# Forgetting attention with its causal mask in the maximum's VectorE pass instead of mask matmuls, and memory tokens multiplied by their factor row at load

## The chip, the cores and the metric

The kernel runs on one core of a Trainium2 chip. A core has a matrix engine (TensorE, PE in the profile; its weight loads are listed as PEld), VectorE (DVE), ScalarE (ACT), GpSimd (POOL) and the queue that issues its transfers (SyncE, SP), which run side by side and wait for one another through semaphores. The time is that of one execution on the device in microseconds. TensorE multiplies a stationary 128x128 tile, loaded as weights, with a moving tile of up to 512 columns; results are summed in PSUM, which has eight banks of 128x512 float32. SBUF is the core's working memory; "DRAM" below means the large memory behind the DMAs.

## The reference, cut to what matters

One decoder layer on 1024 tokens of 1024 features. Four mLSTM heads and eight heads of forgetting attention read the same normalised input; then follow cross-attention into 256 memory tokens and a squared-ReLU MLP. The two parts that the change touches:

```python
def rmsnorm(x, g):
    y = xf * lax.rsqrt(jnp.mean(xf * xf, axis=-1, keepdims=True) + EPS)
    return (y * g.astype(jnp.float32)).astype(x.dtype)

def forgetting_attention(q, k, v, lf):          # per block of 128 queries
    s = jnp.einsum('bqhd,bkhd->bhqk', qi, k) * scale
    s = s + (ci[..., :, None] - cT[..., None, :])
    s = jnp.where(qpos[:, None] >= kpos[None, :], s, -jnp.inf)
    p = jax.nn.softmax(s, axis=-1)
    return jnp.einsum('bhqk,bkhd->bqhd', p.astype(v.dtype), v)

# cross-attention's keys and values, with h = rmsnorm(mem, ln_mem):
k, v = jnp.split(memn @ w_kv, 2, axis=-1)
```

## The kernel before

All activations lie with features on the partitions: x is [128, 8, 1024], eight blocks of 128 features by 1024 tokens. Every float32 product is made of three matmuls on halves: `split` makes a high part (an ACT copy into the matmul's format, L132 or, with a scale, L135) and the remainder as a low part (a DVE subtraction, L133, or with a scale L136), and `mm3` issues low x high, high x low and high x high (L184, L185, L186).

The stages in order: the first norm and the first values (0 to about 63 us), the mLSTM heads with their input projections (to about 380), forgetting attention (about 358 to 600), output projection, cross-attention and MLP (to the end). Outside forgetting attention a planner of the program builder sets each engine's order. It weighs when operands and buffers are ready; `tc.issue_after` only sets the earliest place. Buffers come from small pools: `w2(tag)` hands out [128, 512] tiles, one or two of each tag, and a tile is handed out again only when the last reader of its former content is done. PSUM tiles go by tags too: three `sc`, one `mm`, one `m2`, two `tp`, one `ov`.

**Forgetting attention** is made of tiles of 128 queries (`Tile`) by up to 1024 keys, in one part up to 512 keys and in two beyond. There are 64 tiles (8 heads x 8 blocks), and their last parts have 128, 256, 384 or 512 columns, 16 of each; 32 tiles have a first part of 512 as well. Each part goes through `score` (two matmuls, L721 and L722, and on a tile's last part a third, L724, which adds the causal mask to the last 128 columns by multiplying a bf16 identity with a bf16 mask), `top` (the negated maximum, L728, on DVE; with two parts also the smaller of the two, L731), `exp` (the exponential on ACT, straight from PSUM, with that maximum as its bias), and `scale` (the division by the sum: L741 and L742 on DVE, the product on POOL). `Values` then turns 128-column pieces of the result (L760, TensorE), splits them and multiplies them with the values (L779).

The order here is written by hand: `slot` issues, for one step, the turn of one piece, the products of an earlier one, the maxima of the part scored in the slot before, the piece's split, the exponentials of the part before that, and the scores of the next part; the rest of the slot is filled with matmuls of other work. `in_order` chains each engine's instructions in the order in which they were written. The filler is made of units: cross-attention's keys (`key_unit`, 8 of them) and values (`value_unit`), and half of the output projection. A key unit's matmuls end in a `sink` that multiplies by the factor row of the memory tokens (L874) into SBUF and, in the slot after, splits; a value unit's sink splits straight out of PSUM, scaled by a factor column (L896).

**The memory tokens** are read by `mem_prepare`, which is called ahead of the mLSTM heads and so planned among them (its loads are issued at 14.8 and near 41 us, the last one, of the row, at 86). It reads four pieces of 128x512 (two blocks of 128 features by 256 tokens each), sums their squares, splits them with their gain and stores both halves to DRAM (`hmd`), from where the filler reads them. From the sums come the norm's factors, as a column (`rcol_m`) and, through `to_row`, as a row copied to all partitions (`row_m`): a transpose on TensorE, an ACT copy, a store to DRAM (L249) and a load that repeats the row (L251).

What stands around it on the queues there: `ml_project` of the first head convolves the keys (`conv_silu`, L495 to L503: the projection's PSUM times a row, four taps of 128x1024 on DVE, L498 and L500, and the gate, L503), projects forgetting attention's queries (`fx_project`, 2 x 24 matmuls, whose results go through DVE, L631), transposes the convolved keys (L516 in `carried`, whose result DVE reads at L518), and convolves the queries (24 matmuls for each half).

## Time and profile before

| | |
|---|---|
| median of 3 runs | 1556.06 us (1556.05 to 1556.83) |
| span of the profiled execution | 1551.3 us |
| TensorE busy | 1512.5 us, 97% |
| VectorE busy | 1115.3 us, 72% |
| ScalarE busy | 721.7 us, 47% |
| GpSimd busy | 474.4 us, 31% |
| DMA | 311.94 MB, 201 GB/s mean |

The span is the time from the first to the last instruction that the profiler recorded, for one execution; the profiled execution has no time of its own beside the span, and the runs' times hold about 5 us more than it, the start and the end of the program. In a timeline a row is: start, duration, engine, line, operation, output<-inputs, shape, and in brackets how long the engine stood idle before it and for whom. "SPq" is the queue that issues transfers. A matmul's duration is its latency: the next one starts before it ends, so what one costs is the step to the start of the next. The same holds, to a smaller degree, on VectorE.

The busy share of each engine in 40 slices of the span, with TensorE's granted clock in tenths:

```profile
PE   8999999999999999999999999989999999999997
DVE  7666676665789874944457988888877777767666
ACT  7324343334787763634443556556555422211234
PEclk9999999999999999999999999999999999999998
```

TensorE is busy in nine tenths or more of nearly every slice. VectorE stands at eight or nine tenths in slices 11 to 14, which are forgetting attention (a slice is 38.8 us).

### The profile page before, as it was taken

The numbers are of one execution on the slowest core, as the hardware profiler recorded it, in microseconds if no ns is written. First come the engines' busy times: TensorE is split into PE (matmuls) and PEld (weight loads), VectorE is DVE, ScalarE is ACT, GpSimd is POOL, SyncE is SP. The second block draws the span as 40 slices with busy tenths as digits, with TensorE's granted clock in tenths as the row PEclk, the third lists the DMA queues.
The fourth block names the chain that finished last, engine by engine and source line by source line (L and its number), as shares of the span: only waits on it lengthen the run. The fifth ranks groups of instructions, "written<-read, shape, count | busy, mean of one in ns | idle before, by whom it ended". The sixth has DMA issues, their size and how long they took to land. (4 is left out here: it accounts for less than half of the span.)

```text
span 1551.3 us, 22016 instructions
## 1 busy us (share of the span) xinstructions
PE 1512.5 (97%) x7729; PEld 1262.4 (81%) x7729; DVE 1115.3 (72%) x1736; ACT 721.7 (47%) x1351; POOL 474.4 (31%) x515
## 2 busy tenths in 40 slices
PE   8999999999999999999999999989999999999997
PEld 8878888889898887788888787777777878888887
DVE  7666676665789874944457988888877777767666
ACT  7324343334787763634443556556555422211234
POOL 0003030413455441511110034444444633333320
PEclk9999999999999999999999999999999999999998
DMA  6422223436878949943344457777777976666623
GB/s 220 122 78 84 99 99 113 130 130 170 253 252 231 296 165 312 321 156 117 115 156 154 145 178 265 277 276 260 269 251 261 387 288 244 238 245 239 243 93 110
DMA packets 122108, 311.94 MB, mean 201 GB/s; under 512 B 13566, under 2 KB 28216, under 8 KB 114060
## 3 DMA queue, kind: packets, MB, share of 16 engines
q1 hardware_dynamic: 121996, 310.52, 57.7%
q8 instruction: 61, 1.00, 0.3%
q14 instruction: 51, 0.42, 0.1%
HBM read 206.42 MB, written 104.05 MB: 200 GB/s over the span
## 5 line engine op out<-in xcount | busy, mean ns | idle before, releaser
L184 PE MATMUL tp<-act,wl 128*128 128x512 f32 (+1 forms) x448 | 177.5, 396 | 6.9 <-DVE r_f L1326 3.8
L185 PE MATMUL tp<-act,wh 128*128 128x512 f32 (+1 forms) x448 | 176.3, 393 | 0.0
L186 PE MATMUL tp<-act,wh 128*128 128x512 f32 (+1 forms) x448 | 175.9, 394 | 0.0
L133 DVE TENSOR_TENSOR wl<-wr,wh 128x1024 fp32r<-128x1024 f32 (+2 forms) x99 | 129.1, 1304 | 27.4 <-ACT wh L132 27.0
L132 ACT ACTIVATE wh<-wr 128x1024 fp32r<-128x1024 f32 (+2 forms) x99 | 99.0, 1000 | 86.8 <-PE tp L186 37.2
L184 PE MATMUL mm<-act,wl 128*128 128x512 f32 (+1 forms) x336 | 130.7, 389 | 3.0 <-DVE r_e L1071 1.5
L186 PE MATMUL mm<-act,wh 128*128 128x512 f32 (+1 forms) x336 | 129.0, 384 | 0.0
L185 PE MATMUL mm<-act,wh 128*128 128x512 f32 (+1 forms) x336 | 128.8, 383 | 0.0
L184 PE MATMUL m<-act,wl 128*128 128x512 f32 (+1 forms) x312 | 120.5, 386 | 1.8 <-DVE wl L133 1.5
L186 PE MATMUL m<-act,wh 128*128 128x512 f32 (+1 forms) x312 | 119.3, 382 | 0.0
L185 PE MATMUL m<-act,wh 128*128 128x512 f32 (+1 forms) x312 | 119.1, 382 | 0.0
L184 PEld LDWEIGHTS tp<-act,wl 128*128 128x128 f32 x448 | 84.7, 189 | 28.0 <-DVE r_f L1326 4.2
L184 PE MATMUL sc<-act,wl 128*128 128x512 f32 (+1 forms) x252 | 99.2, 394 | 5.3 <-DVE r_f L1326 3.4
L186 PEld LDWEIGHTS tp<-act,wh 128*128 128x128 f32 x448 | 84.7, 189 | 19.5
L1410 POOL TENSOR_TENSOR z<-wr 128x256 f32<-128x256 f32 x56 | 50.7, 924 | 161.9 <-DMA wr<-w_ff2q 146.2
L185 PEld LDWEIGHTS tp<-act,wh 128*128 128x128 f32 x448 | 84.8, 189 | 18.8
L132 ACT ACTIVATE w<-wr 128x768 fp32r<-128x768 f32 (+2 forms) x31 | 25.6, 826 | 157.5 <-PE tp L186 90.1
L185 PE MATMUL sc<-act,wh 128*128 128x512 f32 (+1 forms) x252 | 98.5, 391 | 0.0
L186 PE MATMUL sc<-act,wh 128*128 128x512 f32 (+1 forms) x252 | 98.3, 390 | 0.0
L132 ACT ACTIVATE wh<-z 128x1024 fp32r<-128x1024 f32 (+1 forms) x54 | 55.4, 1027 | 56.0 <-POOL z L1410 22.2
L133 DVE TENSOR_TENSOR wl<-z,wh 128x1024 fp32r<-128x1024 f32 (+1 forms) x54 | 73.5, 1362 | 6.1 <-ACT wh L132 5.9
L184 PEld LDWEIGHTS mm<-act,wl 128*128 128x128 f32 x336 | 63.3, 188 | 16.9 <-DVE r_e L1071 1.9
(676 smaller groups left out, 4242.1 us busy)
## 6 DMA issues: line engine op xcount, KB each, us to landing
act<-right SPq DMA_DIRECT2D x49, 1024.0 KB
right<-w SPq DMA_DIRECT2D x56, 256.0 KB
wr<-w_ff2q SPq DMA_DIRECT2D x28, 512.0 KB
right<-r_d SPq DMA_DIRECT2D x49, 256.0 KB
right<-r_e SPq DMA_DIRECT2D x49, 256.0 KB
act<-fqk SPq DMA_DIRECT2D x48, 256.0 KB
wr<-w_in SPq DMA_DIRECT2D x20, 512.0 KB
wr<-w_ff SPq DMA_DIRECT2D x20, 512.0 KB
```

What stands on the lines that cost most here:

```text
L132: s.activation(hi, src, AF.Copy)
L133: return v.tensor_tensor(out=lo, in0=src, in1=hi.bitcast(F32), op=ALU.subtract)
L184: nc.tensor.matmul(ps, w[1], x[0], start=first, stop=False, skip_group_check=more)
L185: nc.tensor.matmul(ps, w[0], x[1], start=False, stop=False, skip_group_check=more)
L186: nc.tensor.matmul(ps, w[0], x[0], start=False, stop=last, skip_group_check=more)
L1410: g.tensor_tensor(out=o, in0=x, in1=y, op=op)
```

## The change

It does three things.

1. The mask matmul (L724) and its bf16 identity go. The mask constant becomes 512 columns wide, zero but for its last 128. On a tile's last part `top` is one `tensor_tensor_reduce` on DVE: it adds the mask's last columns (as many as the part has) to the scores in PSUM, multiplies by -1, writes the result back over the scores and keeps the minimum, starting from the first part's result where there is one. The exponential of such a part takes scale -1. The separate minimum (L731) goes.
2. `mem_prepare` runs in two passes: it loads the four pieces and sums squares; makes the factor columns and the row, which is now a `w2("y")` tile; then loads the four pieces again, multiplies them by gain and row in one DVE operation for each half, and splits and stores them.
3. With the factor inside the memory tokens, the key sink is a split straight from PSUM, without the multiplication and without the slot in between, and the value sink splits without a scale.

```diff
@@ -117,11 +117,9 @@
     g.memset(ident, 1.0)
     g.affine_select(out=ident, in_=ident, pattern=[[-1, P]], compare_op=ALU.is_equal, fill=0.0, base=0, channel_multiplier=1)
     BF16 = mybir.dt.bfloat16
-    identb = const("identb", [P, P], BF16)
-    v.tensor_copy(identb, ident)
-    causal = const("causal", [P, P], BF16)
+    causal = const("causal", [P, TH], BF16)
     g.memset(causal, 0.0)
-    g.affine_select(out=causal, in_=causal, pattern=[[-1, P]], compare_op=ALU.is_ge, fill=-BIG, base=0, channel_multiplier=1)
+    g.affine_select(out=causal, in_=causal, pattern=[[-1, TH]], compare_op=ALU.is_ge, fill=-BIG, base=TH - P, channel_multiplier=1)
     half = const("half", [P, 8])
     g.memset(half, -0.5)
     vec = const("vec", [P, a["vec"].shape[1]])
@@ -274,24 +272,29 @@
     vxd = dram.tile([XH, P, 2, 2, NM], F32, name="vxd")
 
     hmd = dram.tile([P, 2, KT, NM], F32, name="hmd")
-    row_m = const("row_m", [P, NM])
-    rcol_m = const("rcol_m", [P, 2])
 
     def mem_prepare():
         acc = w2("b")
+        pairs_of = lambda t: t.rearrange("p (k c) -> p k c", k=2)
         for i in range(KT // 2):
             raw = w2("f")
-            load(raw.rearrange("p (k c) -> p k c", k=2), a["mem"][:, 2 * i : 2 * i + 2])
+            load(pairs_of(raw), a["mem"][:, 2 * i : 2 * i + 2])
             square_sum(acc, raw, i == 0)
+        cols = col("fac", 2)
+        rsqrt_sums(acc, cols, 2, 2)
+        row_m = w2("y")[:, :NM]
+        to_row(row_m, cols, 2, rowd[1:2, :NM])
+        for i in range(KT // 2):
+            raw = w2("f")
+            load(pairs_of(raw), a["mem"][:, 2 * i : 2 * i + 2])
             hi = w2("p", dt=F32R)
             for e in range(2):
                 c = slice(e * NM, e * NM + NM)
                 gain = vec[:, VEC["ln_mem"] + 2 * i + e :][:, 0:1]
-                split(hi[:, c], raw[:, c].bitcast(F32R), raw[:, c], gain)
+                v.scalar_tensor_tensor(out=raw[:, c], in0=raw[:, c], scalar=gain, in1=row_m, op0=ALU.mult, op1=ALU.mult)
+            split(hi, raw.bitcast(F32R), raw)
             for p_, t in enumerate((hi.bitcast(F32), raw)):
-                load(hmd[:, p_, 2 * i : 2 * i + 2], t.rearrange("p (k c) -> p k c", k=2))
-        rsqrt_sums(acc, rcol_m, 2, 2)
-        to_row(row_m, rcol_m, 2, rowd[1:2, :NM])
+                load(hmd[:, p_, 2 * i : 2 * i + 2], pairs_of(t))
 
 
     xa = act(F32)
@@ -719,19 +722,28 @@
             c2 = max(c1, c0 + 256)
             sp = sc()
             nc.tensor.matmul(sp[:, : c2 - c0], qs2[:, it], kl[:, c0:c2], start=True, stop=False)
-            nc.tensor.matmul(sp[:, : c2 - c0], qs[:, it], kh[:, c0:c2], start=False, stop=c1 < self.wid)
-            if c1 == self.wid:
-                nc.tensor.matmul(sp[:, c1 - c0 - P : c1 - c0], identb, causal, start=False, stop=True)
+            nc.tensor.matmul(sp[:, : c2 - c0], qs[:, it], kh[:, c0:c2], start=False, stop=True)
             self.ps.append(sp[:, : c1 - c0])
 
         def top(self, e):
-            v.tensor_reduce(out=self.mxs[:, e : e + 1], in_=self.ps[e], axis=mybir.AxisListType.X, op=ALU.max, negate=True)
-            if e:
-
-                v.tensor_tensor(out=self.mxs[:, 1:2], in0=self.mxs[:, 0:1], in1=self.mxs[:, 1:2], op=ALU.min)
+            ps = self.ps[e]
+            if e + 1 < len(self.parts):
+                v.tensor_reduce(out=self.mxs[:, e : e + 1], in_=ps, axis=mybir.AxisListType.X, op=ALU.max, negate=True)
+            else:
+
+                v.tensor_tensor_reduce(
+                    out=ps,
+                    in0=ps,
+                    in1=causal[:, TH - ps.shape[1] :],
+                    scale=-1.0,
+                    scalar=self.mxs[:, 0:1] if e else BIG,
+                    op0=ALU.add,
+                    op1=ALU.min,
+                    accum_out=self.mxs[:, e : e + 1],
+                )
 
         def exp(self, e):
-            s.activation(self.pt[:, slice(*self.parts[e])], self.ps[e], AF.Exp, bias=self.mxs[:, e : e + 1], accum_out=self.dens[:, e : e + 1])
+            s.activation(self.pt[:, slice(*self.parts[e])], self.ps[e], AF.Exp, bias=self.mxs[:, e : e + 1], scale=1.0 if e + 1 < len(self.parts) else -1.0, accum_out=self.dens[:, e : e + 1])
             if e:
                 s.activation(self.mxs[:, 0:1], self.mxs[:, 0:1], AF.Exp, bias=self.mxs[:, 1:2], scale=-1.0)
 
@@ -870,14 +882,9 @@
                 yield 1.5, k == KT - 1, lambda: sink(ps)
 
         def sink(ps):
-            t = rotate("p", "a").rearrange("p (e c) -> p e c", e=2)
-            v.tensor_tensor(out=t[:, 1], in0=ps[:, :NM], in1=row_m, op=ALU.mult)
-
-            def store():
-                split(t[:, 0].bitcast(F32R), t[:, 1].bitcast(F32R), t[:, 1])
-                load(kxd[n // 2, :, :, n % 2], t)
-
-            return store
+            t = rotate("p", "a").bitcast(F32R).rearrange("p (e c) -> p e c", e=2)
+            split(t[:, 0], t[:, 1], ps[:, :NM])
+            load(kxd[n // 2, :, :, n % 2], t.bitcast(F32))
 
         return [a["w_xk"][n]], run
 
@@ -893,7 +900,7 @@
 
         def sink(t, ps):
             o = rotate("p", "a").bitcast(F32R).rearrange("p (e c) -> p e c", e=2)
-            split(o[:, 0], o[:, 1], ps, rcol_m[:, t : t + 1])
+            split(o[:, 0], o[:, 1], ps)
             load(vxd[hd, :, :, t], o.bitcast(F32))
 
         return [a["w_xv"][hd, i] for i in range(2)], run
```

Line numbers in the changed program differ by a little: L516, L518, L503 and L631 of before are L519, L521, L506 and L634, L728 is L731, and `split`'s subtraction L133 is L131; `mm3` is L182 to L184. The new DVE pass is L734, the multiplication of a memory piece L294.

In the instruction rows below, names carry a running number for each buffer, and the brackets list whom an instruction waits for.

VectorE in forgetting attention, three tiles of the second half of a head. Before, each part has a reduction, and a two-part tile a minimum:

```order
L728 TENSOR_REDUCE c_mx_3235<-sc_3237 128x1 [waits PE_49]
L742 RECIPROCAL c_den_3212<-c_den_3212 128x1
L136 SCALAR_TENSOR_TENSOR r_b_3655<-tp_3630,rcol,r_b_3655 128x4x64 [waits Activation_49]
L728 TENSOR_REDUCE c_mx_3246<-sc_3248 128x1 [waits PE_49]
L742 RECIPROCAL c_den_3226<-c_den_3226 128x1
L728 TENSOR_REDUCE c_mx_3246<-sc_3255 128x1 [waits PE_49]
L731 TENSOR_TENSOR c_mx_3246<-c_mx_3246 128x1 [waits DVE_49]
L742 RECIPROCAL c_den_3236<-c_den_3236 128x1 [waits Activation_49]
```

VectorE at the same place after the change:

```order
L734 ISA sc_3240,c_mx_3238<-sc_3240,causal 128x512 [waits PE_49]
L734 ISA c_mx_3238 128x1
L754 RECIPROCAL c_den_3217<-c_den_3217 128x1
L134 SCALAR_TENSOR_TENSOR r_b_3648<-tp_3623,rcol,r_b_3648 128x4x64 [waits Activation_49]
L731 TENSOR_REDUCE c_mx_3248<-sc_3250 128x1 [waits PE_49]
L754 RECIPROCAL c_den_3230<-c_den_3230 128x1
L734 ISA sc_3257,c_mx_3248<-sc_3257,causal,c_mx_3248 128x128 [waits DVE_49,PE_49]
L734 ISA c_mx_3248 128x1
L754 RECIPROCAL c_den_3239<-c_den_3239 128x1 [waits Activation_49]
```

The last part's reduction is the pair L734, a pass over the scores and an accumulator read; the first part's reduction stays, and the minimum is gone.

TensorE from the end of `fx_project` of the first head on (its last matmul writes a `tp` bank). Before; `m_113` is the bank of the query convolution, `mm_988` that of the transposed keys, `mm_1095` that of a later projection:

```order
L186 MATMUL tp_952<-act_91,wh_916 128x512
L184 MATMUL m_113_1028<-act_89,wl_1023 128x512 [waits DVE_49]
L185 MATMUL m_113_1028<-act_90,wh_1022 128x512
...
L516 MATMUL mm_988<-ident,z_91_905 128x128 [waits DVE_49]
L516 MATMUL mm_988<-ident,z_91_905 128x128 x3
L184 MATMUL mm_1095<-act_89,wl_1092 128x512 [waits DVE_49]
```

TensorE there after the change, where these banks are `m_119`, `mm_994` and `mm_1101`:

```order
L184 MATMUL tp_958<-act_87,wh_922 128x512
L519 MATMUL mm_994<-ident,z_97_911 128x128 [waits DVE_49]
L519 MATMUL mm_994<-ident,z_97_911 128x128 x3
L182 MATMUL mm_1101<-act_85,wl_1098 128x512 [waits DVE_49]
L183 MATMUL mm_1101<-act_86,wh_1097 128x512 [waits Activation_49]
...
L534 MATMUL tp_1005<-ones,r_c_999 128x1 x4
L182 MATMUL m_119_1034<-act_85,wl_1029 128x512 [waits DVE_49]
```

The query convolution's first block of 24 matmuls, which stood between the projection and the key transposes, now follows a later projection.

VectorE at the same place. Before, between the last tap of the key convolution (`z_91_905`) and the operation that frees the transposes' bank (L518):

```order
L500 SCALAR_TENSOR_TENSOR z_91_905<-z_88_851,vec,z_91_905 128x1024 [waits DVE_49]
L503 SCALAR_TENSOR_TENSOR z_91_905<-z_88_851,z_91_905 128x1024 [waits Activation_49]
L631 SCALAR_TENSOR_TENSOR r_p_977<-tp_952,row 128x512 [waits DMAHW5_49,DMAHW3_49,PE_49]
L133 TENSOR_TENSOR wl_1174<-wr_1171,wh_1173 128x1024 [waits DMAHW1_49,Activation_49]
L136 SCALAR_TENSOR_TENSOR w_84_844<-z_91_905,w_83_843 128x1024 [waits Activation_49]
L133 TENSOR_TENSOR r_p_977<-r_p_977,r_p_979 128x512 [waits Activation_49]
L495 TENSOR_TENSOR z_112_1026<-m_113_1028,row 128x512 [waits PE_49]
L518 TENSOR_TENSOR r_c_993<-mm_988,c_m_984 128x512 [waits PE_49]
```

VectorE there after the change (`r_f` are the pieces of the memory tokens, `r_y` the factor row):

```order
L503 SCALAR_TENSOR_TENSOR z_97_911<-z_94_857,vec,z_97_911 128x1024 [waits DVE_49] x3
L294 SCALAR_TENSOR_TENSOR r_f_811<-r_f_811,vec,r_y_805 128x256 [waits DMAHW6_49,DMAHW5_49,Activation_49]
...
L294 SCALAR_TENSOR_TENSOR r_f_820<-r_f_820,vec,r_y_805 128x256
L506 SCALAR_TENSOR_TENSOR z_97_911<-z_94_857,z_97_911 128x1024 [waits Activation_49]
L131 TENSOR_TENSOR r_f_811<-r_f_811,r_p_813 128x512 [waits Activation_49]
L131 TENSOR_TENSOR r_f_820<-r_f_820,r_p_822 128x512 [waits Activation_49]
L521 TENSOR_TENSOR r_c_999<-mm_994,c_m_990 128x512 [waits PE_49]
```

Four multiplications of memory pieces, which wait for the row's load, now stand ahead of the key convolution's gate (L506), and two splits of pieces ahead of L521; the results of `fx_project` (L631 before) have moved behind them.

## The prediction

> **What bounds the kernel now.** I read the page's first part, then the windows (busy time of each engine in the stage that changes), then TensorE's own waits, longest first.

> ```profile
> span 1551.3 us, 22016 instructions
> PE 1512.5 (97%) x7729; PEld 1262.4 (81%) x7729; DVE 1115.3 (72%) x1736; ACT 721.7 (47%) x1351; POOL 474.4 (31%) x515
> ```

> ```profile
> core 0: us, PE busy (x) PEld busy (x) DVE busy (x) ACT busy (x) POOL busy (x), PEclk, DMA share, GB/s
> 410.00:560.00 150.00, 148.68 (x1014) 130.73 (x1013) 130.13 (x318) 117.55 (x325) 76.39 (x119) 1.00 0.80 245
> ```

> ```profile
> PE mm L184 <- DVE wl L133: 6.9, 1, 6.9
> PE m L184 <- DVE act L136: 1.2, 1, 1.2
> PE mm L184 <- DVE r_c L518: 0.9, 1, 0.9
> ```

> TensorE is the bound: 1512.5 of 1551.3 us, and in the core of forgetting attention 148.68 of 150. The stage is packed: what leaves TensorE's queue there shortens the kernel, unless the engine behind it cannot follow. That one is VectorE: 130.13 of 150, so 20 us are idle. TensorE's waits are few: 6.9 us at the very start, which the change leaves alone, and two of about 1 us, at 46.98 and 95.17, both beside the memory work that is rewritten. The median of the runs, 1556.06, is 4.8 us above this profiled span; I make the sum against the span and add the same 4.8 us.

> **Term 1, the mask products go.** 64 bf16 matmuls of 128 columns, one behind each tile's last score part. First the group, then two pieces of TensorE's timeline: a part without mask and a part with it.

> ```profile
> L724 PE MATMUL sc<-causal,identb x64: 229/229/233, 358.7 to 564.7; 128*128 128x128 bf16 x64
> ```

> ```profile
> 455.60 0.39 PE L722 MATMUL sc<-act 128*128 128x512 f32 x1
> 455.83 0.28 PE L184 MATMUL m<-act,wl 128*128 128x256 f32 x1
> 455.94 0.28 PE L185 MATMUL m<-act,wh 128*128 128x256 f32 x1
> ...
> 466.77 0.40 PE L722 MATMUL sc<-act 128*128 128x512 f32 x1
> 467.01 0.23 PE L724 MATMUL sc<-causal,identb 128*128 128x128 bf16 x1
> 467.05 0.36 PE L184 MATMUL m<-wh,act 128*128 128x256 f32 x1
> 467.25 0.28 PE L185 MATMUL m<-wl,act 128*128 128x256 f32 x1
> ```

> The group's 229 ns is a latency, and matmuls overlap, so I don't multiply by it (64 x 0.229 = 14.7 us would be too much). What the mask costs the queue is the step from L722's start to the second matmul behind it. Without mask: 455.94 - 455.60 = 0.34. With mask: 467.25 - 466.77 = 0.48. Between pairs of equal widths I find 0.13 us. 64 x 0.13 = 8.3; a few masks stand ahead of value transposes, which wait for their weight load anyway, so I count 61: **-7.9 us**. Bounds: 0, if TensorE then waits for VectorE instead, and -14.7.

> **Term 2, VectorE takes the mask over.** Each last part's maximum becomes one pass that adds the mask, negates, writes back and takes the minimum; the built program issues two instructions for it, the pass and a 128x1 read of its accumulator. The 32 first parts keep their reduction, and the 32 small minimum operations (L731) go, since the first part's result enters as the starting value. No row of before shows the new pass. The nearest rows, by form in the window 400 to 590 and in the timeline:

> ```profile
> L728 DVE TENSOR_REDUCE c_mx<-sc 128x1 f32<-128x512 f32 x42 | 28.6, 681 | 0.2
> L133 DVE TENSOR_TENSOR r_e<-tp,r_d 128x512 fp32r<-128x512 f32 x32 | 21.9, 685 | 6.5 <-ACT r_d L132 6.2
> L136 DVE SCALAR_TENSOR_TENSOR r_a<-m,rcol_m,r_a 128x256 fp32r<-128x256 f32 x4 | 1.9, 484 | 0.3 <-ACT r_a L135 0.3
> L874 DVE TENSOR_TENSOR r_a<-m,row_m 128x256 f32<-128x256 f32 x4 | 1.6, 408 | 0.0
> ```

> ```profile
> 441.56 0.16 DVE L731 TENSOR_TENSOR c_mx<-c_mx 128x1 f32<-128x1 f32 x1
> 441.63 0.55 DVE L133 TENSOR_TENSOR r_e<-tp,r_d 128x384 fp32r<-128x384 f32 x1
> ...
> 442.43 0.40 DVE L874 TENSOR_TENSOR r_p<-mm,row_m 128x256 f32<-128x256 f32 x1
> 442.75 0.68 DVE L728 TENSOR_REDUCE c_mx<-sc 128x1 f32<-128x512 f32 x1
> 443.35 0.41 DVE L133 TENSOR_TENSOR r_e<-tp,r_d 128x256 fp32r<-128x256 f32 x1
> ```

> A reduction from PSUM (681 ns) and a two-source operation with one source in PSUM (685) cost the same at 512 columns, and the next one starts 0.60 us after either. So I price the pass like the reduction that it replaces. A 128x1 operation takes its neighbour 0.07 us (441.56 to 441.63); a column operand adds 0.06 to 0.08 (484 against 408 at 256 columns). Balance over the stage: 64 accumulator reads x 0.07 = +4.5 (with 0.16, the full latency, +10); 32 starting columns x 0.06 = +1.9; 32 minima x 0.07 = -2.2; that is +4, at most +10. Eight key sinks lose the multiplication by the row (0.32 each, 442.43 to 442.75) and keep their split, -2.6; value sinks lose a column operand, -0.4. Net about +1 us on an engine with 20 idle. The idle time covers it; if that cover were gone, each us more on VectorE would be a us on the kernel. What is left is delay: the exponential starts one accumulator read later (0.1 us), and the key sink's split now reads PSUM twice, so its bank is free one ScalarE copy later (about 0.3 us), where a column of matmuls waits. I take **+0.5** (0 to +1.5) of new waits.

> **The half-rate bound.** If the pass ran at half rate it would take another 0.33 us on a mean tile (320 of 512 columns x 0.53 us, where 0.53 is what 512 columns take within 0.60). 47 of the 64 tiles lie in the 150 us (64 x 150/206): +15.5 on VectorE, while the window shrinks by 47 x 0.13 = 6. 130 + 15.5 + 4 = 150 in 144: VectorE would be the bound. The turning point is 20/47 = 0.43 us per tile, accumulator read included. The row of a two-source pass that has both sources in SBUF speaks against half rate:

> ```profile
> 38.51 0.88 DVE L136 SCALAR_TENSOR_TENSOR r_f<-r_f,vec,r_p 128x256 fp32r<-128x256 f32 x2
> ```

> Two of them take 0.88, 0.40 or so each from start to start, near the 0.33 with a PSUM source. But none of these rows has an accumulator. [...]

> **Term 3, the memory preparation in two passes.** Before: 4 loads, each squared and split at once. Now: 4 loads and squares; then the factor row (a transpose, a 1 KB store, a broadcast load); then 4 more loads, 8 multiplications by gain and row on VectorE, 4 splits, 8 stores. That adds 4 loads of 256 KB on SP's queue, 8 x 0.40 us on VectorE and exchanges 16 half-width operations for 8 full ones. None of it is needed before forgetting attention, 250 us later; what counts is what stands behind it on VectorE's queue. These rows are TensorE at 44 to 96 us, SP, and what a load takes from issue to its first user:

> ```profile
> 46.98 0.38 PE L184 MATMUL m<-wh,act 128*128 128x256 f32 x1 [1.16 <-DVE act L136]
> ...
> 87.80 0.39 PE L186 MATMUL tp<-act,wh 128*128 128x512 f32 x1
> ...
> 93.62 0.60 PE L516 MATMUL mm<-ident,z 128*128 128x128 f32 x4
> ...
> 95.17 0.50 PE L184 MATMUL mm<-act,wl 128*128 128x512 f32 x1 [0.94 <-DVE r_c L518]
> ```

> ```profile
> 40.35 0.33 SPq L284 DMA_DIRECT2D r_f<-mem  x1
> ...
> 84.32 0.26 SPq L249 DMA_DIRECT2D rowd<-row_m  x1
> ...
> 85.98 0.32 SPq L251 DMA_DIRECT2D row_m<-rowd  x1
> ...
> 179.64 0.33 SPq L251 DMA_DIRECT2D r_a<-facd  x1
> ...
> 195.30 0.32 SPq L634 DMA_DIRECT2D fqk<-r_p  x1
> ```

> ```profile
> 44.31 0.63 ACT L220 ACTIVATE r_c<-r_f 128x512 f32<-128x512 f32 x1 [2.07 <-DMA r_f<-mem]
> ```

> ```profile
> 87.39 1.23 DVE L503 SCALAR_TENSOR_TENSOR z<-z,z 128x1024 f32<-128x1024 f32 x1 [1.19 <-ACT z L502]
> ...
> 182.76 0.75 DVE L618 SCALAR_TENSOR_TENSOR r_f<-r_f,vec,r_a 128x512 f32<-128x512 f32 x1 [2.03 <-DMA r_a<-facd]
> ...
> 197.40 0.69 DVE L631 SCALAR_TENSOR_TENSOR r_p<-m,row 128x512 f32<-128x512 f32 x1 [1.40 <-DMA fqk<-r_p]
> ```

> So a memory load takes 4.0 us (40.35 to 44.31), a broadcast row 3.1 (179.64 to 182.76), a store before its buffer may go 2.1 (195.30 to 197.40).

> At 46.98 the wait came from a memory piece that was loaded late, since its buffers had to come free; with pass 1 only squaring, it is loaded earlier, and the wait should go: 1.16 plus the restart, **-1.3** (0 to -1.4).

> At 88 us the order is worse than before. Then a block of 24 matmuls (the query convolution's, 88.03 to 93.6) stood between forgetting attention's query projection and the transposes L516 of the convolved keys, so VectorE had 5.6 us to finish these keys. Now the transposes (L519 in the new numbering) come directly behind the projection, and VectorE has, ahead of the operation that they wait for, four of the new multiplications, which wait for the broadcast row. The factor columns come about 2 us earlier than before (they stand ahead of one 128x1024 pass that they had followed), so the row's load is issued near 83.9 (1.66 after its store, as 84.32 to 85.98) and lands near 87.0; 4 x 0.40 to 88.6, then the 128x1024 pass (1.23 at 87.39) to 89.9. TensorE, at the end of its projection at 88.0, waits 1.9. Then the transposes' consumer stands behind two splits of 0.60 each: 1.5 lost in place of 1.1. The block that was the cover follows later, and needs a PSUM bank that VectorE's L634 frees, which stands behind the third and fourth memory piece: store issued at 90.3, load at 92.3, landed at 96.3, two pieces multiplied and L634 done at 100.4, against TensorE's arrival near 99: 1.4 (0.7 to 1.7). Perhaps one wait more behind it, 0 to 1.5. Together 1.9 + 0.4 + 1.4 and 0 = **+3.5** after rounding down (0, if the loads come a little earlier, to +6). VectorE's queue, not the DMAs, carries the cost: SP is idle most of this time.

> **The sum.** -7.9 + 0.5 - 1.3 + 3.5 = -5.2. Span 1551.3 - 5.2 = 1546.1, with 4.8 outside 1550.9: I say 1551.0.

> **The clock.** A long wait can cost more than itself: behind a wait of 2.78 us a 512-column matmul took 0.67 in place of 0.39, and the granted clock of the next us was 0.50; for some eight matmuls that is 1.7 us lost (8 x 0.21).

> ```profile
> 1020.31 0.67 PE L184 MATMUL sc<-act,wl 128*128 128x512 f32 x1 [2.78 <-DVE r_f L1326]
> ```

> ```profile
> 1021.00:1022.00 1.00, 1.00 (x3) 0.77 (x3) 1.00 (x3) 0.78 (x2) 0.47 (x1) 0.50 0.99 367
> ```

> The waits that I expect at 88 to 99 us are below 2 us each, so I charge nothing. [...]

> **Rivals.**
> - *Early waits with a clock loss* (the memory rewrite costs all it can). Place: 88 to 100 us, price +6 and 1.7 for the clock, no gain at 46.98: -7.9 + 0.5 + 7.7 = +0.3, 1556.4: within 0.2%. For it: both waits hang on VectorE's single queue. Against: the row is needed only late in it.
> - *VectorE becomes the bound* (slower). Place: 380 to 565 us, from 0.43 us more per tile on. At half rate the excess is 6 us in the window, 8 in the stage, and VectorE's waits for ScalarE, which its 20 idle us are, do not vanish (6.2 of them alone before one group of splits): 4 to 8 of the 20 stay. So VectorE's work ends 8 + 6 = 14 us after TensorE's shortened queue: -7.9 + 14 + 2.2 = +8, about 1564. [...] For: the second instruction, no row of the form.
> - *The product was nearly free* (its 128 columns fill time in which the next weights are loaded): -3 in place of -7.9, so 1556. Against: the 0.34 and 0.48 above.
> - *No early cost* (the row lands by 86, as SP is free): -7.9 + 0.5 - 1.3 + 0.5, 1547.9.

> **How the numbers follow.** A measurement of this kernel tells about 0.2%, 3.1 us, from no change: faster is below 1552.95, slower above 1559.2. Forecast, 1549 to 1553: 0.46. No early cost, 1546.5 to 1549: 0.17. Early waits with clock loss: 0.13. Product nearly free: 0.08. VectorE as the bound: 0.16, three quarters of it above 1559.2. Faster: 0.17 and all but 0.01 of the 0.46, 0.62, with 0.02 of the early rival 0.64; slower 0.12, with 0.04 of the early rival for a wait that I did not follow, 0.16; same 0.20. Range 1546.5 to 1559: below it 0.03, above it 0.16. The likeliest case's own range is 1549 to 1553.

> **What would show it.** In the profile after: no bf16 matmul of L724, TensorE busy some 8 us less between 358 and 565; the step from L722 to the second matmul behind it 0.34 everywhere; the new pass near 0.68 us at 512 columns, its accumulator read near 0.16; VectorE near 90% of the window 410 to 554, TensorE still above 98%. Near 47 us no wait; near 88, 91 and 99 us three waits for VectorE of 1 to 2 us. I am wrong if the pass takes 1.1 us at 512 columns and TensorE waits for ScalarE's exponentials or for the score banks; if the waits at 88 us pass 2.8 us and the matmuls behind them take twice their time; or if the order that I read makes waits in places that I did not follow.

## The result, and the profile after

| | before | after |
|---|---|---|
| median | 1556.51 us (20 runs) | 1556.82 us (20 runs) |
| span of the profiled execution | 1551.3 us | 1558.0 us |
| TensorE busy | 1512.5 us | 1509.0 us |
| VectorE busy | 1115.3 us | 1112.8 us |

The ratio is 1.0006 (95% interval 0.9997 to 1.0015): +0.9 us, which can't be told from none. The forecast, 1551.0, was 5.8 us below the time; its range, 1546.5 to 1559.0, holds it, but its likeliest case, 1549 to 1553, doesn't, and "faster", which had the chance 0.64, didn't come. Single executions of one kernel spread by about 4 us on either side (1551.75 to 1559.38 before, 1552.25 to 1560.92 after), and the two profiled ones lie 6.7 us apart, much more than the medians. An execution's time is 1.7 us more than its own span here (1559.74 against 1558.0), so the span of 1551.3 us belongs to a quick execution of about 1553.0, an estimate; start and end of the program are 1.7 us and not the 5 said above. So a profile's end says little here; what says more is the length of a stage between two fixed instructions, and a wait that comes back in several profiles.

The page's first part after:

```profile
span 1558.0 us, 21935 instructions
PE 1509.0 (97%) x7665; PEld 1263.1 (81%) x7665; DVE 1112.8 (71%) x1763; ACT 719.7 (46%) x1347; POOL 475.9 (31%) x515
```

TensorE has 64 matmuls less and still ends later. The window of the stage that changed, with the columns of the window shown of before:

```profile
410.00:560.00 150.00, 144.90 (x987) 131.69 (x986) 122.52 (x336) 118.89 (x328) 78.86 (x125) 1.00 0.84 252
```

TensorE now is idle for 5.1 us of the 150, where it was for 1.3. VectorE isn't fuller (122.5, where it was 130.1), which speaks against it as what TensorE waits for; a kernel below settles that. The transfers' share has risen from 0.80 to 0.84. TensorE's waits, those that are new or matter below:

```profile
PE sc L724 <- ACT act L746: 4.4, 4, 2.2
...
PE m L182 <- POOL wl L954: 2.7, 1, 2.7
...
PE mm L519 <- DVE z L506: 1.9, 1, 1.9
...
PE mm L182 <- DVE r_c L521: 1.1, 1, 1.1
...
PE m L182 <- DVE r_p L634: 0.9, 1, 0.9
```

The last three are those foreseen at 88, 91 and 99 us. The first two, 7.1 us together, are in forgetting attention and in the filler behind it, and weren't foreseen. The new VectorE pass itself, by form in the window 400 to 590:

```profile
L731 DVE TENSOR_REDUCE c_mx<-sc 128x1 f32<-128x512 f32 x28 | 19.1, 682 | 0.1
L734 DVE DVE_READ_ACCUMULATOR2_ANT c_mx<- 128x1 f32 x57 | 7.7, 136 | 0.1
L734 DVE CUSTOM_DVE_ANT_0 sc<-sc,causal,c_mx 128x512 f32<-128x512 f32 x8 | 6.0, 752 | 0.2
L734 DVE CUSTOM_DVE_ANT_0 sc<-sc,causal 128x512 f32<-128x512 f32 x7 | 4.8, 681 | 0.0
```

The pass takes 681 ns at 512 columns, the reduction that stayed 682; the starting column costs 71 ns more, and the accumulator read 136. So it is as fast as the reduction that it replaces.

**The early part.** TensorE, then VectorE, then the granted clock:

```profile
89.85 0.66 PE L519 MATMUL mm<-ident,z 128*128 128x128 f32 x4 [1.94 <-DVE z L506]
91.65 0.62 PE L182 MATMUL mm<-act,wl 128*128 128x512 f32 x1 [1.15 <-DVE r_c L521]
...
101.65 0.50 PE L182 MATMUL m<-act,wl 128*128 128x512 f32 x1 [0.85 <-DVE r_p L634]
```

```profile
86.98 1.67 DVE L294 SCALAR_TENSOR_TENSOR r_f<-r_f,vec,r_y 128x256 f32<-128x256 f32 x4 [2.90 <-DMA r_y<-rowd]
88.58 1.22 DVE L506 SCALAR_TENSOR_TENSOR z<-z,z 128x1024 f32<-128x1024 f32 x1
```

```profile
92.00:93.00 1.00, 1.00 (x4) 0.50 0.65 242
93.00:94.00 1.00, 1.00 (x4) 0.50 0.34 111
94.00:95.00 1.00, 1.00 (x3) 0.50 0.78 137
```

The factor row lands at 86.98, the four multiplications end at 88.6 and the gate L506 starts then; TensorE waits 1.94, 1.15 and 0.85 us. Behind the second wait the granted clock is 0.50 for 3.4 us (91.88 to 95.29): nine matmul steps are too long by 1.6 us together. Between the two waits TensorE had only the four key transposes, from 89.85 on. From 63 us to 159 us of before (two fixed instructions, the factor row's first product and the second head's last key transpose), the changed kernel lost 4.9 us.

### The profile page after: what moved, and what is told of

The parts are those of the page before. It is cut to its first block, busy times and chain, and to the rows that moved or that the text cites. A ratio compares the mean times of both kernels' runs of the same rounds, so it can differ in the third digit from the quotient of the medians.

```text
span 1558.0 us, 21935 instructions
## 1 busy us (share of the span) xinstructions
PE 1509.0 (97%) x7665; PEld 1263.1 (81%) x7665; DVE 1112.8 (71%) x1763; ACT 719.7 (46%) x1347; POOL 475.9 (31%) x515
## 5 line engine op out<-in xcount | busy, mean ns | idle before, releaser
L182 PE MATMUL tp<-act,wl 128*128 128x512 f32 (+1 forms) x448 | 177.4, 396 | 6.2 <-DVE r_f L1333 3.5
L184 PE MATMUL tp<-act,wh 128*128 128x512 f32 (+1 forms) x448 | 175.9, 394 | 0.0
L131 DVE TENSOR_TENSOR wl<-wr,wh 128x1024 fp32r<-128x1024 f32 (+2 forms) x99 | 128.2, 1296 | 28.4 <-ACT wh L130 28.3
L182 PE MATMUL mm<-act,wl 128*128 128x512 f32 (+1 forms) x336 | 130.0, 387 | 3.1 <-DVE r_e L1078 1.5
L184 PE MATMUL mm<-act,wh 128*128 128x512 f32 (+1 forms) x336 | 129.6, 386 | 0.0
L182 PE MATMUL m<-act,wl 128*128 128x512 f32 (+1 forms) x312 | 119.5, 383 | 5.6 <-POOL wl L954 2.7
L184 PE MATMUL m<-act,wh 128*128 128x512 f32 (+1 forms) x312 | 119.2, 382 | 0.0
L182 PEld LDWEIGHTS tp<-act,wl 128*128 128x128 f32 x448 | 84.7, 189 | 27.2 <-DVE r_f L1333 4.0
L182 PE MATMUL sc<-act,wl 128*128 128x512 f32 (+1 forms) x252 | 99.4, 394 | 5.5 <-DVE r_f L1333 3.6
L184 PEld LDWEIGHTS tp<-act,wh 128*128 128x128 f32 x448 | 84.8, 189 | 19.4
L184 PE MATMUL sc<-act,wh 128*128 128x512 f32 (+1 forms) x252 | 98.2, 390 | 0.0
L182 PEld LDWEIGHTS mm<-act,wl 128*128 128x128 f32 x336 | 63.5, 189 | 17.7 <-DVE r_e L1078 1.9
L131 DVE TENSOR_TENSOR wl<-z,wh 128x1024 fp32r<-128x1024 f32 (+1 forms) x54 | 72.9, 1349 | 5.6 <-ACT wh L130 5.5
```

Source lines behind the costliest of these rows:

```text
L131: return v.tensor_tensor(out=lo, in0=src, in1=hi.bitcast(F32), op=ALU.subtract)
L182: nc.tensor.matmul(ps, w[1], x[0], start=first, stop=False, skip_group_check=more)
L184: nc.tensor.matmul(ps, w[0], x[0], start=False, stop=last, skip_group_check=more)
```

## The experiments

Twelve kernels ran. Their times stand beside runs of the kernel before on the same chip:

| kernel | ratio to before | 95% interval | us of 1556 |
|---|---|---|---|
| mask part alone | 0.9984 | 0.9975 to 0.9993 | -2.5 |
| the same again | 0.9981 | 0.9971 to 0.9992 | -3.0 |
| memory part alone | 1.0048 | 1.0032 to 1.0063 | +7.5 |
| no mask at all | 0.9985 | 0.9976 to 0.9995 | -2.3 |
| changed kernel again | 1.0016 | 1.0005 to 1.0028 | +2.5 |
| mask part, weights not reloaded | 0.9918 | 0.9902 to 0.9934 | -12.8 |
| before, weights not reloaded | 0.9961 | 0.9947 to 0.9975 | -6.1 |
| second pass later | 1.0101 | 1.0083 to 1.0119 | +15.7 |
| mask part, half loads | 0.9973 | 0.9963 to 0.9983 | -4.2 |
| before, half loads | 1.0001 | 0.9990 to 1.0011 | +0.2 |
| row product on GpSimd | 1.0000 | 0.9992 to 1.0009 | 0.0 |

The twelfth is a single execution of the kernel before, for its profile, 1555.68 us.

Two measures come from the profiles of all of them. The length of forgetting attention is the time from TensorE's first score (L721, 358.45 in the kernel before) to the 177th of its 192 value products (L779, 577.84; the last one starts at 586.19), against the 219.4 us of before. The stalls are the steps between TensorE instructions, from that first score to 26 us behind that product (about where the filler ends), that are more than 0.2 us longer than the median step of their kind, summed.

| profile | stage, us against before | stalls, us |
|---|---|---|
| before; again | 0; +0.6 | 3.9; 5.6 |
| before, weights not reloaded | -0.2 | 3.4 |
| before, half loads | +0.1 | 5.5 |
| changed; again | -0.5; -4.2 | 13.0; 8.7 |
| mask part alone; again | -4.1; -3.9 | 8.3; 8.6 |
| no mask at all | -1.9 | 10.3 |
| mask part, weights not reloaded | -6.6 | 4.9 |
| mask part, half loads | -4.0 | 8.9 |
| memory part alone | +0.3 | 4.5 |
| second pass later | -4.7 | 8.7 |
| row product on GpSimd | -1.1 | 11.0 |

### One part of the change at a time

The mask part alone keeps the memory preparation of before; its factor row waits in DRAM and is loaded into the free `row` tile when forgetting attention begins, since the wider mask takes the room.

```diff
@@ mask part alone: top(), score() and exp() as in the change, and
-        to_row(row_m, rcol_m, 2, rowd[1:2, :NM])
+        ps = ov_()
+        nc.tensor.transpose(ps[:2, :P], rcol_m, ident)
+        t = w2("y")
+        s.activation(t[:2, :P], ps[:2, :P], AF.Copy)
+        load(rowd[1:2, :NM].rearrange("o (t q) -> (o t) q", t=2), t[:2, :P])
...
     load(hm.bitcast(F32), hmd)
+    load(row[:, :NM], rowd[1:2, :NM].broadcast_to([P, NM]))
```

> The mask part alone: maximum and mask in one VectorE pass, the memory tokens prepared once as before (the factor row waits in DRAM and is loaded into a free row when forgetting attention begins). Theory A (the mask part gains what the products cost, the memory rewrite gives it back at 88 to 103 us): 6 to 8 us faster than before, ratio 0.995 to 0.996, no wait of TensorE above 1.2 us at 85 to 105 us. Theory B (forgetting attention ends on its transfers, so a shorter TensorE queue waits for late weights and rows): at most 3 us faster, ratio 0.998 or above, with ScalarE waiting longer for weight loads in 400 to 600. Theory C (VectorE's pass is too slow to hide): slower or equal, VectorE above 95% busy there.

The memory part alone is the change without its hunks in `Tile` and in the mask constant:

> The memory part alone: two passes over the memory tokens and direct splits in the sinks, mask products kept. Theory A: 4 to 7 us slower than before, ratio 1.003 to 1.0045, with the three waits of TensorE at 88, 91 and 101 us and half clock behind the second. Theory B: 0 to 3 us slower, since waits in the early part would be made up later by transfers that are then on time. Theory C: 4 to 7 us slower too.

No mask at all:

```diff
-            nc.tensor.matmul(sp[:, : c2 - c0], qs[:, it], kh[:, c0:c2], start=False, stop=c1 < self.wid)
-            if c1 == self.wid:
-                nc.tensor.matmul(sp[:, c1 - c0 - P : c1 - c0], identb, causal, start=False, stop=True)
+            nc.tensor.matmul(sp[:, : c2 - c0], qs[:, it], kh[:, c0:c2], start=False, stop=True)
```

> The kernel before without its mask products and with nothing in their place: the causal mask is left out, so all keys of a tile count. It prices the products alone. Theory A: 7 to 8.5 us faster, ratio about 0.995. Theory B: at most 3 us faster, since the stage ends on its transfers. Theory C: 7 to 8.5 us faster, clearly more than the kernel with the mask on VectorE.

And the changed kernel once more:

> The changed kernel once more, for a second profile beside the first: which waits come back. Theory A: waits at 88, 91 and 101 us and the half clock again, 1556 to 1558 us; the long waits at 393, 471 and 606 us (1.3, 2.2 and 2.7) smaller or elsewhere, as they hang on transfers that landed late in one execution. Theory B: the waits at 393, 471 and 606 us come back at their places and sizes.

Measured: the mask part gains 2.5 us and the memory part costs 7.5, of which 4.5 lie in the part from 63 to 159 us of its profile. Theory A is right on the memory part and wrong on the mask part. Without any mask and with no VectorE work in its place, the gain is 2.3 us, no more than with the mask on VectorE. So VectorE's pass costs nothing that can be seen (the two gains agree within their intervals, about 1.4 us to either side each), and theory C falls; what keeps the gain small isn't VectorE, and theory B stands. The price of one product was right: over the 63 of 64 parts with the same neighbours and no wait in both profiles, the step from L722 to the second matmul behind it, the product not counted, is 0.126 us shorter in the median, 7.8 to 7.85 us in sum, by the profile that is compared. The gain is made and then waited away: the stalls lie at 3.4 to 5.6 us in the profiles with the products and, the kernel without reloads (below) apart, at 8.3 to 13.0 in those without them, with the memory part or with that of before.

The second profile of the changed kernel has the waits at 88, 90 and 101 us again (2.07, 1.14, 1.26) and half clock twice: the granted clock is 0.50 from 89.24 to 96.07, so from behind the first of them on, and from 102.89 to 106.31, behind the third (2.5 and 1.5 us lost). The wait at 471 us came back as one of 1.40 us, behind a wait of ScalarE of 3.28 for the same kind of load, and the one at 606 as 2.06; that at 393 did not.

### Do the transfers hold the shorter stage?

In the first profile of the changed kernel the wait at 471 us reads so; TensorE, then ScalarE:

```profile
471.15 0.50 PE L724 MATMUL sc<-act 128*128 128x512 f32 x1 [2.15 <-ACT act L746]
```

```profile
469.53 0.63 ACT L953 ACTIVATE wh<-wr 128x512 fp32r<-128x512 f32 x1 [3.98 <-DMA wr<-w_xv]
```

The exponential (L746) that frees TensorE's score bank stands on ScalarE's queue behind the cut of a weight tile that hasn't landed. There are two raw buffers for these weights, and one is reloaded only when both of its halves have been cut. ScalarE had such a wait in the profile of before too, at 462.76:

```profile
462.76 0.63 ACT L946 ACTIVATE wh<-wr 128x512 fp32r<-128x512 f32 x1 [2.03 <-DMA wr<-w_xv]
```

To take these loads away without moving an instruction of the engines, the next two kernels load the buffers twice and then cut the same contents again, which leaves out every later load of the filler's weights:

```diff
-            raw = sb("wr", [P, 1024], 2)[:, : src.shape[-1]]
-            last_raw[:] = [load(raw, src)]
-            raws_.append(raw)
+            if n < 2:
+                raw = sb("wr", [P, 1024], 2)
+                last_raw[:] = [load(raw[:, : src.shape[-1]], src)]
...
+            else:
+                raws_.append(whole[n % 2][:, : src.shape[-1]])
```

> The mask part alone, and the filler's weights in forgetting attention are loaded only twice: every later unit cuts and multiplies the same two raw buffers again (so cross-attention's keys and values and half of the output projection are made with wrong weights; all other work is issued as in the mask part alone). Theory B (the shorter stage waits for its weight loads, 2.9 to 4.3 us each on ScalarE, and TensorE behind them): 4 to 7 us faster than before, ratio 0.9955 to 0.9975, no wait near 463 us and less than 0.5 us near 597. Theory D (the new waits come from VectorE and GpSimd slowing one another, not from transfers): the same as the mask part alone, ratio 0.9984, the waits in place.

> The kernel before with the filler's weights loaded only twice in the same way (wrong weights there too), mask products kept. Theory B: 0 to 1 us faster than before, since with the products in its queue TensorE came late enough for the loads. Theory D: the same time.

ScalarE's waits for transfers of weights in 400 to 612 us, first in the mask part alone, then without the reloads:

```profile
ACT wh L956 <- DMA wr<-w_out_a: 3.2, 1, 3.2
ACT wh L956 <- DMA wr<-w_xv: 2.9, 1, 2.9
ACT wh L956 <- DMA wr<-w_xk: 0.6, 1, 0.6
```

```profile
ACT wh L130 <- DMA wr<-w_out_b: 4.1, 1, 4.1
```

And TensorE where the filler ends, in the same two:

```profile
597.01 0.47 PE L182 MATMUL m<-act,wl 128*128 128x512 f32 x1 [1.68 <-DVE r_a L926]
```

```profile
594.14 0.47 PE L182 MATMUL m<-act,wl 128*128 128x512 f32 x1 [0.31 <-DVE r_a L926]
```

Without the reloads the mask part is 6.7 us faster than the kernel before is without them (12.8 against 6.1; the interval of each is some 2.5 us to either side), near the 7.85 of the products, and the stalls are 4.9 us against 3.4. With the reloads it is 2.5. So by the times the weight loads take some 4 of the 7 us, a difference that is good to about 4 us; by the stage's length, where the mask part gains 4.1 us with the loads and 6.6 without, they take 2.5. Theory D of these two kernels, by which the time would stay the same, falls. That the kernel before also gains 6 was missed by theory B, which had said 0 to 1: hardly any of it lies in forgetting attention (0.2 us), 3.7 between its end and 676 us, where its waits at 637 and 651 us (1.5 and 1.6) are gone or below 0.4.

Is it when these loads are issued, or what they move? Half loads issue each half of a buffer as soon as that half has been cut:

```diff
+    def half_load(n, e):
+        if n < len(sources):
+            src = sources[n][1]
+            w = src.shape[-1] // 2
+            last_raw[:] = [load(whole[n % 2][:, e * w : (e + 1) * w], src[:, e * w : (e + 1) * w])]
...
         halves[0] += 1
+        half_load(n + 2, e)
```

> The mask part alone, and the filler's two raw weight buffers are refilled by halves: each half is loaded as soon as that half has been cut, in place of the whole buffer after its second half. Theory B (the stage waits for late weight loads): ScalarE's waits for w_xv and w_out_a (2.9 and 3.2 us in the mask part alone) fall below 2 each, 1 to 4 us faster than the mask part alone, ratio to before 0.996 to 0.998. Theory D (the loads are limited by the bytes that all transfers move, not by when they are issued): the same as the mask part alone, 0.9984.

> The kernel before, mask products kept, with the filler's raw weight buffers refilled by halves. If half loads help by themselves (0.1% in the mask part), 1 to 2 us faster, ratio 0.9987 to 0.9994; if they help only a stage that the shorter TensorE queue has made wait (theory B in its strict form), the same as before, 1.000.

> The mask part alone once more, on the same chip as the run above. Theory B expects 0.9984 again (0.9975 to 0.9993) and waits of ScalarE for w_xv and w_out_a of about 3 us each; above 0.9995 the gain of the mask part alone would not be settled.

The mask part with half loads is at 0.9973, the fastest that computes everything and faster than both kernels; its wait for w_xv fell from 2.9 to 1.0, but that says little, since the waits for w_out_a are 7.6 us in sum where the mask part's two profiles have 3.2 and 7.4, and the stalls didn't fall. On the kernel before, half loads change nothing (1.0001). Against the mask part alone (0.9984, 0.9981 on another occasion) the gain of 1 us isn't clear of its interval. So an earlier issue helps a little at most, and only the shorter stage; whether the rest is bytes (the share was 0.84 in the window above) or the order on the queue stays open.

The kernel before, profiled again:

> The kernel before once more for a second profile: theory A and B both expect the wait at 463 us below 0.3 us and that at 600 us below 0.7; if they come out above 0.8 and 1.8, those waits are no mark of the shorter stage.

Its wait at 465 us is 0.24 us, that at 601 is 1.55. The second is nearly as long as in some kernels without products (1.68 with the mask part alone), so this wait alone marks nothing; the sum of the stalls does.

### What the second pass over the memory tokens costs, and where

```diff
     ready = ml_project(0)
+    mem_scale()
```

Here `mem_scale` is the second pass (row load, four loads, multiplications, splits, stores), cut off from `mem_prepare`, which ends with the store of the row.

> The changed kernel with only its second pass over the memory tokens called later, behind the first head's projections; it loads the factor row from DRAM there. Theory A (the pass costs by its place on VectorE's queue at 82 to 103 us): no wait of TensorE above 1.2 us in 85 to 105 us, 4 to 7 us faster than the changed kernel, ratio to before 0.997 to 0.999, near the mask part alone. Rival E (its 4 MB of loads and stores or its VectorE work cost wherever they stand): ratio 1.0 to 1.002.

The waits at 88 to 103 us are gone, as theory A has it: from 63 to 155 us TensorE has none above 0.2 us. And it is 15.7 us slower than before, where theory A had it faster than before and rival E nearly level. The place is now 154 to 164 us; TensorE, then VectorE, then TensorE's window:

```profile
156.02 1.11 PE L527 MATMUL tp<-ident,z 128*128 128x128 f32 x4 [4.64 <-DVE z L514]
164.31 0.80 PE L182 MATMUL tp<-act,wl 128*128 128x512 f32 x1 [7.18 <-DVE r_p L642]
```

```profile
153.95 0.88 DVE L302 SCALAR_TENSOR_TENSOR r_f<-r_f,vec,r_y 128x256 f32<-128x256 f32 x2 [5.04 <-DMA r_f<-mem]
154.75 1.22 DVE L514 SCALAR_TENSOR_TENSOR z<-z,z 128x1024 f32<-128x1024 f32 x1
...
162.77 0.88 DVE L302 SCALAR_TENSOR_TENSOR r_f<-r_f,vec,r_y 128x256 f32<-128x256 f32 x2 [3.33 <-DMA r_f<-mem]
163.57 0.68 DVE L642 SCALAR_TENSOR_TENSOR r_p<-tp,row 128x512 f32<-128x512 f32 x1
```

```profile
158.00:162.00 4.00, 0.00 (x0) 0.50 0.43 103
```

The planner set multiplications of memory pieces ahead of the next head's gate and of a projection's result, and the pieces landed 5 and 3 us after VectorE stood there. It is the same mechanism, with a later piece in place of the row, and the granted clock is 0.50 from 154.02 to 167.67 us: each piece's buffer comes free only when the former piece's halves are stored.

The other way is to take the row product off VectorE:

```diff
-                v.scalar_tensor_tensor(out=raw[:, c], in0=raw[:, c], scalar=gain, in1=row_m, op0=ALU.mult, op1=ALU.mult)
-            split(hi, raw.bitcast(F32R), raw)
+                g.tensor_tensor(out=raw[:, c], in0=raw[:, c], in1=row_m, op=ALU.mult)
+                split(hi[:, c], raw[:, c].bitcast(F32R), raw[:, c], gain)
```

> The changed kernel with the memory tokens' multiplication by the row on GpSimd, and the gain back in the split (8 half-width splits). Theory A (TensorE waits at 88 us because VectorE's queue stands at the multiplication until the row has landed): the wait of 1.9 us for L506 at 88 to 90 us goes or falls below 0.6, since nothing that waits for the row stands ahead of it any more; a wait behind the transposes stays, because a split of a memory piece still stands ahead of L521. Ratio to before 0.999 to 1.002. Rival E (the wait comes from the amount of VectorE work, not from the row): 1.5 to 2 us at the same place, ratio 1.001 to 1.003.

TensorE, VectorE and GpSimd there:

```profile
90.08 0.50 PE L182 MATMUL mm<-act,wl 128*128 128x512 f32 x1 [2.43 <-DVE r_c L521]
```

```profile
84.58 1.23 DVE L506 SCALAR_TENSOR_TENSOR z<-z,z 128x1024 f32<-128x1024 f32 x1 [1.19 <-ACT z L505]
...
87.47 1.95 DVE L134 SCALAR_TENSOR_TENSOR r_f<-r_f,vec,r_p 128x256 fp32r<-128x256 f32 x2 [1.67 <-ACT r_p L133]
89.34 0.68 DVE L521 TENSOR_TENSOR r_c<-mm,c_m 128x512 f32<-128x512 f32 x1
```

```profile
86.15 2.99 POOL L294 TENSOR_TENSOR r_f<-r_f,r_y 128x256 f32<-128x256 f32 x4 [10.30 <-DMA r_y<-rowd]
```

The gate L506 now runs at 84.58, and its wait is gone. One wait stays, behind the split of the first piece, which has the row's landing behind it by way of GpSimd. It is one wait of 2.43 us, and it brings half clock too, from 90.79 to 94.20 us (columns: window, TensorE's busy time, granted clock, the transfers' share, GB/s):

```profile
90.00:91.00 1.00, 0.92 (x4) 0.90 0.69 262
91.00:92.00 1.00, 1.00 (x4) 0.50 0.00 0
```

About 1.1 us of the wait is a new cost: the two half-width splits ahead of it take 1.95 us together while GpSimd is at work, where the two at 91.08 and 92.61, with GpSimd idle, take 0.47 each. The part from 63 to 159 us costs 4.0 us in place of 4.9 and 7.9 in the two profiles of the changed kernel, and the kernel is level with before. So the wait for the row is moved and shortened more than removed, and the gain over the changed kernel (1.0016 and 1.0006 to 1.0000) is hardly clear of the intervals. This kernel alone doesn't rule out rival E, since VectorE's work on the pieces is less too (4.7 us busy in place of 6.1). What speaks against E is the row of VectorE at 86.98 above: the engine stood idle for 2.90 us until the factor row had landed, with the gate behind it on its queue.

## Why the prediction was right or wrong

**Right:** the price of the products (7.9 us; 7.85 by steps). The pass like the reduction that it replaces (681 against 682 ns), the starting column at 0.06 (0.07), and with it no half rate, which no row of before had shown for a pass with an accumulator. The wait at 46.98 went. The early chain came as worked out: the row at 86.98 (87.0), the multiplications to 88.6 (88.6), waits of 1.94, 1.15 and 0.85 (1.9, 1.5, 1.4), and that the cost sits on VectorE's queue, shown by its 2.90 us of idle time ahead of the gate and by the kernel that moved the pass and its waits.

**Wrong, first and largest: the new waits of +0.5 (0 to +1.5).** The step that failed is the one behind it, in what bounds the kernel: "what leaves TensorE's queue there shortens the kernel, unless the engine behind it cannot follow. That one is VectorE". What couldn't follow were, for the larger part, the weight loads, behind which ScalarE's exponentials stand. Measured: 3 to 9 us more stalls in the stage, 4.1 us gained of 7.9 with the mask part alone, and 6.6 without the reloads, where +1.3 of new waits are left, inside the bounds that I gave for VectorE's side. The window that I quoted had the transfers' share at 0.80, and ScalarE already waited 2.03 us for a load of w_xv at 462.76 in the profile of before (the row above), hidden from TensorE then. I read the waits of TensorE alone, and took the idle time of one engine for the slack of the stage.

| waits, us | profile | share of the stretch | clock behind it |
|---|---|---|---|
| 1.94 at 90 and 1.15 at 92 | changed | 0.07 | 0.50 |
| 2.07 at 89 | changed, again | 0.24 | 0.50 |
| 2.43 at 90 | row product on GpSimd | 0.21 | 0.50 |
| 2.15 at 471 | changed | 0.46 | 1.00 |
| 2.68 at 606 | changed | 0.47 | 1.00 |

The last two are as long as those above them, but a boundary of the grid falls into each, so that matmuls fill nearly half of the stretch. The term that was put at nothing is the half clock behind 88 us: 1.6 us in the first profile, 2.5 and 1.5 in the second.

With the transposes counted too, the highest share ahead of half clock is 0.40 in these profiles and the lowest ahead of full clock 0.47, so whether they count is not shown. The matmuls of less than 64 columns are left out because the stretch of 0.40 would be at 0.63 with its eight of one column (L534), and half clock came behind it all the same.

So the term of the memory part, +2.2 net, was 3.6 and 6.6 in the two profiles of the changed kernel (4.9 and 7.9 less the 1.3 at 46.98), 3.2 in that of the memory part alone (4.5 less 1.3), and by its time alone 7.5 (5.0 to 9.8). The sum by measured parts, -2.5 and +7.5, is +5.0; the changed kernel was at +0.9 (-0.5 to +2.3) and +2.5 (+0.8 to +4.4). The parts don't add up within about 3 us, and I can't say where; the stages behind 848 us, whose TensorE instructions are the same, move by as much between executions (against the profile of before, 3.0 us longer with the memory part alone, 3.0 shorter in the second profile of the changed kernel).

The rival "early waits with a clock loss" gave 1556.4, close to the time, but only half for its reason: it had the full gain of the products. That the range holds the time is in part luck: both errors went the same way, and what took in their 5.8 us is the room that the range left for other cases.

One sum of the prediction was off without effect: the turning point of the half-rate bound, 20/47 = 0.43 us per tile, leaves out the 6 us by which the window shrinks; with them it is 14/47 = 0.30. As the pass ran as fast as the reduction, nothing hung on it.

Open: why VectorE waited 4.09 us for the load of a factor row at 390 us in the first profile of the changed kernel and 2.24 in the second; whether bytes or order make the late weight loads.

## What to carry to other kernels

Before crediting what leaves the bound engine's queue, ask of every engine what it waits for in that stage, transfers first: a wait that costs nothing today (ScalarE's 2.0 us for a weight load) is the next bound. An operation that waits for a transfer must not stand on an in-order queue ahead of work that TensorE needs soon; moving it later by the planner's own estimate can make it worse (15.7 us), while giving it to another, idle engine shortens the wait and here brought the kernel level with before. For the clock, don't go by the longest wait: ask how little of any 3.41 us the matmuls of 64 columns and more around a group of waits may cover; in the stretches measured here 0.40 or less was followed by half clock, 0.46 or more was not.
